# A hybrid attention layer on one core: two gate sums, the latents' last steps and the fetches of o's blocks at other places

## The chip, the cores and the metric

The kernel runs on one core of a Trainium2 chip. The metric is the device time of one execution in microseconds (us). A core has a matrix engine (TensorE, PE, with its weight loads as PEld), three engines for elementwise work (VectorE or DVE, ScalarE or ACT, GpSimd or POOL) and SyncE (SP), which here issues most of the DMA transfers. Each engine works through its own list of instructions in order; semaphores make one wait for another. PE adds its products up in banks of PSUM, and a bank can be written anew only when its last reader is done.

## The reference

The layer has 512 tokens of width 2048, in float32: RMSNorm, one wide input projection, two groups of eight attention heads side by side (MLA with latents of width 768 and 512 and a shared rotary key of 64; FoX with a forget gate), a SiLU gate on each group, one output projection, RMSNorm and the residual.

```python
h = _rms_norm(x, g_pre)
proj = h @ w_in
(q_lat, kv_lat, k_rope_raw, gate_mla,
 fq, fk, fv, f_logit, gate_fox) = jnp.split(proj, split_points, axis=-1)
o_mla = _mla_branch(q_lat, kv_lat, k_rope_raw, g_q, w_uq, g_kv, w_ukv, cos, sin) * jax.nn.silu(gate_mla)
o_fox = _fox_branch(fq, fk, fv, f_logit, b_forget) * jax.nn.silu(gate_fox)
o = jnp.concatenate([o_mla, o_fox], axis=-1) @ w_out
return x + _rms_norm(o, g_post)
```

In the MLA branch the latents are normalised (`_rms_norm(q_lat, g_q)`, `_rms_norm(kv_lat, g_kv)`) and projected to queries of 8 x 192 and to keys and values of 8 x 256; causal softmax attention follows in blocks of 128 queries.

## The kernel before

**Arithmetic.** Every float32 operand is split into a high and a low part that PE takes (`split`, `divide`: a cast on ACT, L129 or L249, then a subtraction on DVE, L130 or L250), and a product is three matmuls, high by high, high by low and low by high (`mm3`, L138 to L140). Weights come in chunks of 128 x 1024. `chunk(i)` hands out chunk i, has chunk i+4 loaded and chunk i+2 divided. There are three buffers each for raw chunks, high parts (`whi`) and low parts (`wlo`). Some chunks come in two parts, `raw` and `second`, which DVE adds ahead of the division (L246).

**Block products.** The columns of the input projection that make the latents ("l", 512 wide) and the MLA gate ("m") are computed by a scheme in the manner of Strassen and Winograd: seven products of half blocks (p1, p2, p4, q6, g5, g7, g3) whose operands are blocks of x (after RMSNorm) and of the weights, or sums of them. The sums of x's blocks were written to memory before. `fetches(n, "m")` issues four loads of 256 KB from there on SP (L908), one per function; the tiles are called `bmg`. `divisions(n, "m")` splits each of them in two. A product is given a list `side`, from which one function is taken every second step of eight; the rest of that list is emptied at the product's end. The output projection is done in the same manner, over the attention's result o; its blocks a11 and a12 come back from memory as `boa`, two loads of 256 KB each, the same L908.

**The order of the stages.** p1, p2 and p4 each for l and m in turn; then q6, g5, g7, g3 for l (504 to 551 us), then the same four for m (551 to 598 us). After that come four pairs of MLA heads, p = 0 to 3. For each pair the queries are projected (`mq`), then keys and values (`mk`, `mv`). The attention of the pair's two heads is put off: its steps (scores of four query blocks, tiles `sm`, exponentials `pm` by L621, transposes `ptm`, values `pvm`) run between the projection steps of the next pair. The output projection follows at about 739 us.

**What sets the order around the change.** Put-off work waits in a queue, `todo`; `pump(n)` takes n functions from it at each step of a product, where n is the product's `rate`. `drain()` runs all that is left. The latents' last steps (scales of their RMSNorm, `latent_part`, L1181) and the gate's parts go through this queue. The gate's sums (`scaled`, L1233, tiles `gc`) combine a product's two banks with an earlier sum, on DVE, and free the banks. `gate(f)` transposes a sum on PE into a bank `gmt` and computes the SiLU. From the program in this order the framework makes each engine's list, and takes an instruction earlier than it is written where it expects it to be ready; so an instruction can stand well ahead of its place in the code. The banks are four for projections (tag pj), three for scores and transposes (at) and one for values (pv).

Of the kernel before, what the change touches and what calls it, by code (L numbers as in the profile page):

```python
# [63 lines left out]
def tile_hybrid_layer(  # L64
# [37 lines left out]
    def proj_bank(name):  # L102
        return bank("pj", name, 4)
# [371 lines left out]
    def drain():  # L475
        while todo:
            todo.popleft()()
# [3 lines left out]
    def set_pace(n):  # L481
        state.update(pace=n, tiles=0)
# [432 lines left out]
    def divisions(n, of):  # L915
        return [lambda j=j: part_fetched(n, of, j) for j in range(2 if of == "o" else 4)]

    def along(a, b):
        return [lambda x=x, y=y: (x(), y()) for x, y in zip(a, b)]

    def fetches(n, of):
        return [lambda j=j: fetch(n, of, j) for j in range(2 if of == "o" else 4)]

    def operand(n, of):
        def parts(kk, t):
            return [oper[n, of][kk // 2][:, x, kk % 2, t * P : (t + 1) * P] for x in range(2)]

        return parts
# [269 lines left out]
    def x_block(half, tokens):  # L1198
        def parts(kk, t):
            ts = slice((tokens + t) * P, (tokens + t + 1) * P)  # L1200
            return hh[8 * half + kk][:, ts], hl[8 * half + kk][:, ts]

        return parts
# [5 lines left out]
    def sums_wide(n):  # L1209
        return lambda kk: [oper[n, "m"][kk // 2][:, x, kk % 2, :] for x in range(2)]  # L1210
# [19 lines left out]
    def scaled(to, o, t0, add, op=ALU.add, col=hcol):  # L1230

        for t in range(2):
            dve.scalar_tensor_tensor(  # L1233
                out=to[:, t, :], in0=o[t], scalar=col[:, t0 + t : t0 + t + 1], in1=add[:, t, :], op0=ALU.mult, op1=op
            )
# [30 lines left out]
    raws_of += [slot(f"lat{i}") for i in range(2)]  # L1266
    for t, to in enumerate(lat_block(0, 0)):
        act.copy(to, fold(A[t]))
    product("p2", "m", x_block(1, 0), A2, False, True)
    c11 = slot("gc11")  # L1270
    scaled_copy(c11, A2, 0)
    B, B2 = ([proj_bank(f"gb{n}{t}") for t in range(2)] for n in "lm")
    product("p4", "l", x_wide(1, 2), B, True, True, side=divisions("q6", "m"), turned=True)
    lat_sum(lat_block(0, 1), B, pl)
    product("p4", "m", x_block(1, 2), B2, True, True, side=fetches("g5", "m"))
    c21 = slot("gc21")
    scaled(c21, B2, 2, pb)
    drain()
    C, G = ([proj_bank(f"g{n}l{t}") for t in range(2)] for n in "cd")
    product("q6", "l", sums_wide("q6"), C, True, True, side=along(divisions("g5", "m"), fetches("g7", "m")), turned=True)  # L1280
    raws_of += [slot(f"lat{i}") for i in (2, 3)]
    lat_sum(lat_block(1, 0), C, pl, ALU.subtract)
    product("g5", "l", sums_wide("g5"), G, True, True, side=along(divisions("g7", "m"), fetches("g3", "m")), turned=True)
    lat_sum(lat_block(1, 1), G, pl, ALU.subtract)
    product("g7", "l", sums_wide("g7"), C, False, True, side=divisions("g3", "m"), turned=True)
    lat_sum(lat_block(1, 1), C, lat_block(1, 1))
    lat_less(lat_block(0, 1), C)
    for i in range(4):
        todo.append(lambda i=i: latent(i, raw(i)))
    product("g3", "l", sums_wide("g3"), G, False, True, turned=True)  # L1290
    lat_sum(lat_block(1, 0), G, lat_block(1, 0))
    for i in range(4, 8):
        todo.append(lambda i=i: latent(i, raw(i)))
# [7 lines left out]
    for i in range(10):  # L1301
        todo.append(lambda i=i: latent_part(i))
    C, G = ([proj_bank(f"g{n}m{t}") for t in range(2)] for n in "cd")
    product("q6", "m", operand("q6", "m"), C, True, True)
    c12 = slot("gc12")
    scaled(c12, C, 0, pa, ALU.subtract)
    product("g5", "m", operand("g5", "m"), G, True, True)
    c22 = slot("gc22")
    scaled(c22, G, 2, pb, ALU.subtract)
    product("g7", "m", operand("g7", "m"), C, False, True)  # L1310
    todo.append(lambda: scaled(c21, C, 2, c21, col=ncol))
    todo.append(lambda: scaled(c22, C, 2, c22))
    for f in range(4):
        todo.append(lambda f=f: gate(f, c11, c21))
    product("g3", "m", operand("g3", "m"), G, False, True)
    drain()
    todo.append(lambda: scaled(c12, G, 0, c12))
    for f in range(4, 8):
        todo.append(lambda f=f: gate(f, c12, c22))
    qnh, qnl = zip(*(latents[i] for i in range(6)))  # L1320
# [2 lines left out]

    for p in range(4):
        c = mla[p]
        if p == 1:
            for f in (*fetches("a11", "o"), *fetches("a12", "o")):
                f()
        if p == 2:
            todo.extendleft([*divisions("a11", "o"), *divisions("a12", "o")])  # L1330
        qb = [proj_bank(f"mq{p}{i}") for i in range(3)]

        proj_T(c["q"], [(qb[i], P, cols(i * P)) for i in range(3)], qnh, qnl, rate=2)
        q = [[split(qb[i], f"mq{p}{i}", SC_M, first=P)] for i in range(2)]
        wholes = slot(f"mw{p}")
        qw = [[whole_block(wholes, i, qb[i], SC_M)] for i in range(2)]
        a, b = rotate(qb[2], P, SC_M, f"q{p}")
        for i in range(2):
            r = tmp(f"rq{p}{i}")
            src = slice(ROPE * i, ROPE * (i + 1))  # L1340
            for half in range(2):
                dve.tensor_tensor(
                    out=r[ROPE * half : ROPE * (half + 1), :], in0=a[src, :], in1=b[src, :], op=ALU.add
                )
            q[i].append(split(r, f"rq{p}{i}", first=P))
            qw[i].append(whole_block(wholes, 4 + i, r))
        if p == 0:
            set_pace(2)
        kb = [proj_bank(f"mk{p}{i}") for i in range(2)]
        vb = [proj_bank(f"mv{p}{i}") for i in range(2)]  # L1350

        def v_cols(w, j):
            return w[:, j, :].rearrange("p (h c) -> p h c", h=2)[:, :, NOPE:]

        kk = 0
        for i in c["kv"]:
            hi, lo = chunk(i)
            for j in range(chunks[i][3]):
                fst, lst = kk == 0, kk == KVR // P - 1
                for n in range(2):  # L1360
                    w = cols(256 * n)
                    mm3(kb[n], w(hi, j), w(lo, j), knh[kk], knl[kk], fst, lst)
                for t in range(NT):
                    o = vb[t // 2][:, (t % 2) * 256 : (t % 2) * 256 + 256]
                    ts = slice(t * P, (t + 1) * P)
                    mm3(
                        o, knh[kk][:, ts], knl[kk][:, ts], v_cols(hi, j), v_cols(lo, j),
                        fst and t % 2 == 0, lst, skip_group_check=True,
                    )
                kk += 1  # L1370
# [16 lines left out]
        enqueue_scores(heads)  # L1387
        enqueue_values(heads)
        done += heads
# [218 lines left out]
```

## Time and profile before

| | us |
|---|---|
| median of 3 runs (914.35 to 918.75) | 918.18 |
| the profiled execution | 916.44 |
| its span, from the first to the last instruction | 914.5 |
| PE busy | 898.6 |
| DVE busy | 626.4 |
| ACT busy | 423.6 |
| POOL busy | 80.5 |
| mean granted clock of PE (1 is full) | 0.996 |

The rows that follow come from the profile of one execution. Times are us from the start of the span unless they are marked ns. A group row names the line, the engine, the operation, the tiles out and in (without numbers), the shapes and the count; then the busy time, the mean ns of one, and the time that the engine was idle just before, with what ended it. A row of the list of waits names the waiting engine and line, the instruction that ended the wait, and the total, the number and the longest. The chain of waits follows the program back from a moment: each row is a start, a duration and what took it. "x8" is a count; SPq is SP's queue of issues. Durations of matmuls overlap, so that PE's pace is read from start to start.

### The profile page before, as it was taken

The numbers are of one execution on the slowest core, as the hardware profiler recorded it, in microseconds if no ns is written. First come the engines' busy times: TensorE is split into PE (matmuls) and PEld (weight loads), VectorE is DVE, ScalarE is ACT, GpSimd is POOL, SyncE is SP. The second block draws the span as 40 slices with busy tenths as digits, with TensorE's granted clock in tenths as the row PEclk, the third lists the DMA queues.
The fourth block names the chain that finished last, engine by engine and source line by source line (L and its number), as shares of the span: only waits on it lengthen the run. The fifth ranks groups of instructions, "written<-read, shape, count | busy, mean of one in ns | idle before, by whom it ended". The sixth has DMA issues, their size and how long they took to land.

```text
span 914.5 us, 12937 instructions
## 1 busy us (share of the span) xinstructions
PE 898.6 (98%) x4732; PEld 774.3 (85%) x4732; DVE 626.4 (69%) x1074; ACT 423.6 (46%) x779; POOL 80.5 (9%) x97
## 2 busy tenths in 40 slices
PE   9999999999999999999999999998999999999997
PEld 8988888898889887888998998877888888888885
DVE  3476878447472764573767777987968896886585
ACT  5772434243221432242554546554554566654473
POOL 1010111111121011011100000001111000000021
PEclk9999999999999999999999999999999999999999
DMA  9378888997997898989789965549999436787878
GB/s 302 93 201 214 232 215 193 239 228 193 225 273 183 199 253 208 235 209 223 249 303 302 305 195 171 163 125 260 206 231 223 119 118 199 239 257 221 271 193 251
DMA packets 121364, 199.40 MB, mean 218 GB/s; under 512 B 16050, under 2 KB 59596, under 8 KB 121300
## 3 DMA queue, kind: packets, MB, share of 16 engines
q1 hardware_dynamic: 105044, 158.84, 55.4%
q0 software_dynamic: 15520, 39.33, 23.4%
q8 instruction: 37, 0.61, 0.3%
q10 hardware_dynamic: 736, 0.40, 0.1%
q14 instruction: 27, 0.22, 0.1%
HBM read 186.46 MB, written 70.80 MB: 281 GB/s over the span
## 4 chain that ended last, share of the span: by engine, by line
PE 55%; DVE 4%; DMA 2%; ACT 1%; issue 0%; SPq 0%; DVEq 0%; ACTq 0%
PE sm L604 2%; PE mq L138 2%; PE mq L140 2%; PE mq L139 2%; PE oa L140 2%; PE oa L138 2%; PE oa L139 2%; PE od L139 2%; PE oc L139 2%; PE od L138 2%; PE oc L140 2%; PE oc L138 2%; PE od L140 2%; DVE wlo L250 1%; DMA boa<-awayoa 1%; PE ptm L630 1%
## 5 line engine op out<-in xcount | busy, mean ns | idle before, releaser
L250 DVE TENSOR_TENSOR wlo<-raw,whi 128x1024 fp32r<-128x1024 f32 (+3 forms) x205 | 242.8, 1186 | 172.8 <-ACT whi L249 163.5
L249 ACT CAST whi<-raw 128x1024 fp32r<-128x1024 f32 (+3 forms) x205 | 209.2, 1022 | 299.7 <-PE fk L139 52.9
L138 PE MATMUL fq<-h,whi 128*128 128x512 f32 x128 | 52.6, 411 | 0.0
L138 PE MATMUL fg<-h,whi 128*128 128x512 f32 x128 | 50.9, 398 | 0.0
L140 PE MATMUL fq<-h,wlo 128*128 128x512 f32 x128 | 50.3, 393 | 0.0
L140 PE MATMUL fg<-h,wlo 128*128 128x512 f32 x128 | 50.1, 392 | 0.0
L139 PE MATMUL fq<-h,whi 128*128 128x512 f32 x128 | 50.1, 391 | 0.0
L138 PE MATMUL fk<-h,whi 128*128 128x512 f32 x128 | 50.0, 391 | 0.0
L139 PE MATMUL fg<-h,whi 128*128 128x512 f32 x128 | 49.9, 390 | 0.0
L139 PE MATMUL fk<-h,whi 128*128 128x512 f32 x128 | 49.8, 389 | 0.0
L140 PE MATMUL fk<-h,wlo 128*128 128x512 f32 x128 | 49.8, 389 | 0.0
L294 POOL DMA_DIRECT2D t<-in_w_out_dram x16 | 18.5, 1159 | 265.0 <-DMA raw<-in_w_uq_dram 177.0
L140 PE MATMUL fv<-whi,h 128*128 128x256 f32 (+1 forms) x128 | 39.5, 309 | 0.0
L138 PE MATMUL fv<-whi,h 128*128 128x256 f32 (+1 forms) x128 | 39.5, 309 | 0.0
L139 PE MATMUL fv<-wlo,h 128*128 128x256 f32 (+1 forms) x128 | 39.5, 309 | 0.0
L561 PE MATMUL fv<-whi,h 128*128 128x456 f32 x128 | 37.6, 378 | 0.0
L138 PE MATMUL mq<-ln,whi 128*128 128x512 f32 x72 | 29.3, 410 | 1.6 <-DVE gc L1233 1.6
L621 ACT ACTIVATE pf<-sf,stf 128x128 f32<-128x128 f32 (+3 forms) x32 | 16.9, 529 | 27.0 <-DVE stf L619 27.0
L139 PE MATMUL mq<-ln,whi 128*128 128x512 f32 x72 | 28.8, 400 | 0.0
L140 PE MATMUL mq<-ln,wlo 128*128 128x512 f32 x72 | 28.8, 400 | 0.0
L140 PEld LDWEIGHTS fq<-h,wlo 128*128 128x128 f32 x128 | 24.0, 188 | 5.4
L140 PEld LDWEIGHTS fg<-h,wlo 128*128 128x128 f32 x128 | 24.0, 188 | 5.3
(525 smaller groups left out, 2452.9 us busy)
## 6 DMA issues: line engine op xcount, KB each, us to landing
raw<-in_w_in_dram SPq DMA_DIRECT2D x80, 512.0 KB
t<-in_w_out_dram SPq DMA_DIRECT2D x32, 512.0 KB
raw<-t SPq DMA_DIRECT2D x32, 512.0 KB
raw<-in_w_out_dram SPq DMA_DIRECT2D x24, 512.0 KB
t<-in_w_out_dram POOLq DMA_DIRECT2D x16, 512.0 KB, 8.7
t<-t POOLq DMA_DIRECT2D x16, 512.0 KB, 8.0
awaymg<-rmg POOLq DMA_DIRECT2D x8, 512.0 KB, 9.1
raw<-t6l SPq DMA_DIRECT2D x8, 512.0 KB
```

The costliest lines, as they stand in the source:

```text
L138: pe.matmul(o, ah, bh, start=first, stop=False, **kw)
L139: pe.matmul(o, ah, bl, start=False, stop=False, **kw)
L140: pe.matmul(o, al, bh, start=False, stop=last, **kw)
L249: act.copy(hi[:, :m], raw[:, :m])
L250: dve.tensor_tensor(out=lo[:, :m], in0=raw[:, :m], in1=hi[:, :m].bitcast(F32), op=ALU.subtract)
L294: pool.dma_start(to.rearrange("p (k c) -> p k c", k=2), second, accum_op=ALU.add)
L561: pe.matmul(banks[t][:, :n], a[k][:, tss[t]], b[:, j, :], start=k == 0 and m == 0, stop=k == NK - 1 and m == 2,)
L604: pe.matmul(s[:, :nn], a[:, qs], c[:, :nn], start=(i == 0), stop=(i == len(pairs) - 1))
L621: act.activation(p, s[:, :n], AF.Exp, bias=st[:, 0:1], accum_out=st[:, 1:2])
L630: pe.transpose(pt[:, b * P : (b + 1) * P], self.p[b][:, n0 : n0 + P], ident)
```

## The change

Four things move; no arithmetic is added or taken away.

1. The fetches and divisions of x's sums are shifted by two: the first two fetches of g5 stand in p2's gate half (`f5[:2]`), the other two and the first two divisions with the first two fetches of g7 in q6 l, and so on, until the last two divisions of g3 stand in g3 l. Before, all four of g5 stood in p4's gate half.
2. The product q6 m takes two functions from `todo` at a step, where it took one.
3. The gate's sums with g7 m and g3 m are computed directly behind their products, where they went through `todo`.
4. The fetches of o's blocks a11 and a12 are issued at the start of pair 3, before at the start of pair 1; their divisions enter `todo` behind pair 3's query projection, before at the start of pair 2.

```diff
-    product("p2", "m", x_block(1, 0), A2, False, True)
+    d5, d7, d3 = (divisions(n, "m") for n in ("g5", "g7", "g3"))
+    f5, f7, f3 = (fetches(n, "m") for n in ("g5", "g7", "g3"))
+    product("p2", "m", x_block(1, 0), A2, False, True, side=f5[:2])
...
-    product("p4", "m", x_block(1, 2), B2, True, True, side=fetches("g5", "m"))
+    product("p4", "m", x_block(1, 2), B2, True, True)
...
-    product("q6", "l", sums_wide("q6"), C, True, True, side=along(divisions("g5", "m"), fetches("g7", "m")), turned=True)
+    product("q6", "l", sums_wide("q6"), C, True, True, side=[*f5[2:], *along(d5[:2], f7[:2])], turned=True)
...
-    product("g3", "l", sums_wide("g3"), G, False, True, turned=True)
+    product("g3", "l", sums_wide("g3"), G, False, True, side=d3[2:], turned=True)
...
-    product("q6", "m", operand("q6", "m"), C, True, True)
+    product("q6", "m", operand("q6", "m"), C, True, True, 2)
...
     product("g7", "m", operand("g7", "m"), C, False, True)
-    todo.append(lambda: scaled(c21, C, 2, c21, col=ncol))
-    todo.append(lambda: scaled(c22, C, 2, c22))
+    scaled(c21, C, 2, c21, col=ncol)
+    scaled(c22, C, 2, c22)
     for f in range(4):
         todo.append(lambda f=f: gate(f, c11, c21))
     product("g3", "m", operand("g3", "m"), G, False, True)
+    scaled(c12, G, 0, c12)
     drain()
-    todo.append(lambda: scaled(c12, G, 0, c12))
...
-        if p == 1:
+        if p == 3:
             for f in (*fetches("a11", "o"), *fetches("a12", "o")):
                 f()
-        if p == 2:
-            todo.extendleft([*divisions("a11", "o"), *divisions("a12", "o")])
...
+        if p == 3:
+            todo.extendleft([*divisions("a11", "o"), *divisions("a12", "o")])
```

(g5 l and g7 l change in the same way as q6 l.)

**Blocks of o, on ACT.** This is ACT's list before, where pair 1's query projection begins; `pm` is the exponential of a score block of pair 0, `mv0h` and `mv` are pair 0's values.

```order
L129 CAST mv0h_5923<-mv_5818 128x256
L129 CAST mv0h_5925<-mv_5819 128x256
L129 CAST boa_5935<-boa_5935 128x512
L1031 COPY mv_5927<-mv_5819 128x256
L129 CAST boa_5937<-boa_5937 128x512
L621 ACTIVATE pm_5967,stm_5965<-sm_5961,stm_5965 128x128
L129 CAST boa_5939<-boa_5939 128x512
L621 ACTIVATE pm_5980,stm_5978<-sm_5971,stm_5978 128x256
L129 CAST boa_5941<-boa_5941 128x512
L249 CAST whi_6027<-raw_5868 128x1024
L621 ACTIVATE pm_6002,stm_6000<-sm_5993,stm_6000 128x384
```

In the list after, this is ACT where pair 3's query projection begins; `pm` and `mv` are pair 2's.

```order
L129 CAST mv2h_6759<-mv_6601 128x256
L633 COPY pdm_6748<-ptm_6746 128x128
L129 CAST boa_6769<-boa_6769 128x512
L129 CAST boa_6771<-boa_6771 128x512
L129 CAST boa_6773<-boa_6773 128x512
L1031 COPY mv_6761<-mv_6601 128x256
L129 CAST boa_6775<-boa_6775 128x512
L621 ACTIVATE pm_6801,stm_6799<-sm_6795,stm_6799 128x128
L249 CAST whi_6858<-raw_6669 128x1024
L621 ACTIVATE pm_6814,stm_6812<-sm_6805,stm_6812 128x256
```

The casts of boa have left the exponentials of pair 0, and all four now stand ahead of the first exponential of pair 2, where two stood ahead of the first of pair 0.

**Blocks of o, on SP.** Before, at the end of pair 2 (`t` is work for the output projection's weights, raw from in_w_ukv pair 3's key and value weights):

```order
L297 DMA t_168<-in_w_out_dram 128x2x512
L299 DMA t_160<-whi_6668 1x16
L234 DMA raw_6666<-in_w_ukv_dram 128x2x512
L297 DMA t_160<-in_w_out_dram 128x2x512
L234 DMA raw_6788<-in_w_ukv_dram 128x2x512
L299 DMA t_164<-whi_6790 1x16
L234 DMA raw_6864<-in_w_out_dram 128x2x512
L297 DMA t_164<-in_w_out_dram 128x2x512
```

After, at the same place:

```order
L297 DMA t_168<-in_w_out_dram 128x2x512
L234 DMA raw_6669<-in_w_ukv_dram 128x2x512
L234 DMA raw_6780<-in_w_ukv_dram 128x2x512
L299 DMA t_160<-whi_6671 1x16
L908 DMA boa_6769<-awayoa_4132 128x512
L908 DMA boa_6771<-awayoa_4005 128x512
L908 DMA boa_6773<-awayoa_4146 128x512
L908 DMA boa_6775<-awayoa_4025 128x512
L297 DMA t_160<-in_w_out_dram 128x2x512
L234 DMA raw_6856<-in_w_out_dram 128x2x512
```

The four fetches stand behind both loads of in_w_ukv, and one 512 KB load of `t` that stood between these two now stands behind the fetches.

**Fetches of x's sums, on DVE.** Before, in p2's gate half and p4's first half (`wlo` with `whi` are the low parts of weight chunks, raw with second the sums of chunks in two parts, `bmg` the blocks of x's sums):

```order
L250 TENSOR_TENSOR wlo_4373<-raw_4312,whi_4372 128x1024
L246 TENSOR_TENSOR raw_4348<-raw_4348,second_4350 128x1024
L250 TENSOR_TENSOR wlo_4394<-raw_4348,whi_4393 128x1024
L246 TENSOR_TENSOR raw_4368<-raw_4368,second_4370 128x1024
L246 TENSOR_TENSOR raw_4388<-raw_4388,second_4390 128x1024
L250 TENSOR_TENSOR wlo_4415<-raw_4368,whi_4414 128x1024
L250 TENSOR_TENSOR wlo_4443<-raw_4388,whi_4442 128x1024
L246 TENSOR_TENSOR raw_4409<-raw_4409,second_4411 128x1024
L250 TENSOR_TENSOR wlo_4478<-raw_4409,whi_4477 128x1024
```

After, at the same place:

```order
L250 TENSOR_TENSOR wlo_4375<-raw_4312,whi_4374 128x1024
L246 TENSOR_TENSOR raw_4348<-raw_4348,second_4350 128x1024
L130 TENSOR_TENSOR bmg_4368<-bmg_4368 128x512
L250 TENSOR_TENSOR wlo_4398<-raw_4348,whi_4397 128x1024
L246 TENSOR_TENSOR raw_4370<-raw_4370,second_4372 128x1024
L130 TENSOR_TENSOR bmg_4390<-bmg_4390 128x512
L250 TENSOR_TENSOR wlo_4419<-raw_4370,whi_4418 128x1024
L246 TENSOR_TENSOR raw_4392<-raw_4392,second_4394 128x1024
L250 TENSOR_TENSOR wlo_4447<-raw_4392,whi_4446 128x1024
L246 TENSOR_TENSOR raw_4413<-raw_4413,second_4415 128x1024
L250 TENSOR_TENSOR wlo_4482<-raw_4413,whi_4481 128x1024
```

Two low parts of bmg stand between the additions and low parts of the chunks that p4 uses.

**Gate sums, on DVE.** Before, at the end of g3 m (`lat` and `ln` are the latents and their parts, `gc` the gate's sums, `gm` the gate):

```order
L130 TENSOR_TENSOR ln_5583<-lat_4805,ln_5583 128x512
L1181 SCALAR_TENSOR_TENSOR lat_3743<-lat_3743,gcol,ls 128x512
L250 TENSOR_TENSOR wlo_5602<-raw_5538,whi_5601 128x768
L130 TENSOR_TENSOR ln_5593<-lat_3743,ln_5593 128x512
L1181 SCALAR_TENSOR_TENSOR lat_3743<-lat_3743,gcol,ls 128x512
L1233 SCALAR_TENSOR_TENSOR gc_4661<-gcm_5210,ncol,gc_4661 128x512
L1233 SCALAR_TENSOR_TENSOR gc_4661<-gcm_5211,ncol,gc_4661 128x512
L130 TENSOR_TENSOR ln_5612<-lat_3743,ln_5612 128x512
L250 TENSOR_TENSOR wlo_5626<-raw_5567,whi_5625 128x768
L1233 SCALAR_TENSOR_TENSOR gc_5443<-gcm_5210,hcol,gc_5443 128x512
L1233 SCALAR_TENSOR_TENSOR gc_5443<-gcm_5211,hcol,gc_5443 128x512
L1251 SCALAR_TENSOR_TENSOR gm_5643<-gm_5643,gmt_5644 128x512
```

After, in g3 m:

```order
L130 TENSOR_TENSOR ln_5515<-lat_3743,ln_5515 128x512
L1181 SCALAR_TENSOR_TENSOR lat_3743<-lat_3743,gcol,ls 128x512
L250 TENSOR_TENSOR wlo_5543<-raw_5492,whi_5542 128x1024
L130 TENSOR_TENSOR ln_5531<-lat_3743,ln_5531 128x512
L1233 SCALAR_TENSOR_TENSOR gc_4657<-gcm_5210,ncol,gc_4657 128x512
L1233 SCALAR_TENSOR_TENSOR gc_4657<-gcm_5211,ncol,gc_4657 128x512
L1233 SCALAR_TENSOR_TENSOR gc_5463<-gcm_5210,hcol,gc_5463 128x512
L1233 SCALAR_TENSOR_TENSOR gc_5463<-gcm_5211,hcol,gc_5463 128x512
L250 TENSOR_TENSOR wlo_5568<-raw_5518,whi_5567 128x1024
L1251 SCALAR_TENSOR_TENSOR gm_5577<-gm_5577,gmt_5578 128x512
L1251 SCALAR_TENSOR_TENSOR gm_5577<-gm_5577,gmt_5591 128x512
L250 TENSOR_TENSOR wlo_5604<-raw_5540,whi_5603 128x1024
```

The four gc that read g7's banks stood among the low parts of pair 0's query weights (768 columns). Now they stand ahead of all of these, and ahead of the last two low parts of 1024 columns.

More of the change, by code (lines that the diff above doesn't have):

```diff
@@ L1279, in tile_hybrid_layer @@
     C, G = ([proj_bank(f"g{n}l{t}") for t in range(2)] for n in "cd")
-    product("q6", "l", sums_wide("q6"), C, True, True, side=along(divisions("g5", "m"), fetches("g7", "m")), turned=True)
+    product("q6", "l", sums_wide("q6"), C, True, True, side=[*f5[2:], *along(d5[:2], f7[:2])], turned=True)
     raws_of += [slot(f"lat{i}") for i in (2, 3)]
     lat_sum(lat_block(1, 0), C, pl, ALU.subtract)
-    product("g5", "l", sums_wide("g5"), G, True, True, side=along(divisions("g7", "m"), fetches("g3", "m")), turned=True)
+    product("g5", "l", sums_wide("g5"), G, True, True, side=[*along(d5[2:], f7[2:]), *along(d7[:2], f3[:2])], turned=True)
     lat_sum(lat_block(1, 1), G, pl, ALU.subtract)
-    product("g7", "l", sums_wide("g7"), C, False, True, side=divisions("g3", "m"), turned=True)
+    product("g7", "l", sums_wide("g7"), C, False, True, side=[*along(d7[2:], f3[2:]), *d3[:2]], turned=True)
     lat_sum(lat_block(1, 1), C, lat_block(1, 1))
```

## The prediction

> **What bounds the kernel now.** I read the page first, then the list of waits of TensorE, then the chain of waits around each entry of that list, and last the table of stretches with their clock. The page says that TensorE is the bound:
>
> ```profile
> span 914.5 us, 12937 instructions
> PE 898.6 (98%) x4732; PEld 774.3 (85%) x4732; DVE 626.4 (69%) x1074; ACT 423.6 (46%) x779; POOL 80.5 (9%) x97
> ```
>
> The program's matrix work does not change, so all that an edit of this kind can win is the time in which PE waits or runs at a lower clock. The list of waits (who waited for what, us in total, times, longest) is short:
>
> ```profile
> PE sm L604 <- ACT pm L621: 2.6, 1, 2.6
> PE mix L1450 <- ACT scaler L1449: 1.9, 1, 1.9
> PE mq L138 <- DVE gc L1233: 1.6, 1, 1.6
> PE gbm L139 <- DVE wlo L250: 1.3, 2, 0.8
> PE xt L423 <- DMA xa<-in_x_dram: 1.1, 1, 1.1
> PE pvf L139 <- DVE plf L130: 0.9, 1, 0.9
> ```
>
> The waits on xt and mix are the program's start and end, which the change does not touch. Three lie in its reach: sm (scores of latent pair 0, run in pair 1's q projection), mq (start of pair 0) and gbm (product p4's gate half). The first is the dearest. The chain of waits there (start, us, what) is:
>
> ```profile
> 625.71 8.54 DMA boa<-awayoa
> ...
> 634.28 0.62 ACT boa L129
> ...
> 635.68 0.37 ACT pm L621 x2
> 636.10 1.77 PE sm L604 x5
> 637.86 0.43 PE mq L138
> ...
> 640.93 0.23 PE mq L140
> ```
>
> A block of o (boa) takes 8.54 us to land. Its cast stands on ACT ahead of the first exponential (pm), ACT works in order, and PE waits for the bank that this exponential frees. A matmul of mq, 0.23 us at the full clock (the last row), takes 0.43 right after the wait. The table of stretches (start:end, length, busy us and count of PE, PEld, DVE, ACT and POOL, granted clock, DMA share, GB/s) says why:
>
> ```profile
> 597.00:600.50 3.50, 2.34 (x16) 1.71 (x14) 3.50 (x6) 3.13 (x4) 0.00 (x0) 1.00 0.44 152
> 600.50:604.00 3.50, 3.10 (x16) 2.59 (x17) 3.50 (x6) 1.79 (x4) 0.00 (x0) 1.00 0.55 152
> ...
> 633.44:636.85 3.41, 0.82 (x4) 0.67 (x4) 1.13 (x3) 2.57 (x8) 0.00 (x0) 1.00 1.11 313
> 636.85:640.27 3.42, 3.42 (x10) 2.60 (x10) 3.32 (x9) 1.66 (x5) 0.00 (x0) 0.52 0.91 250
> ```
>
> PE was busy for 0.82 of 3.41 us, and in the next 3.42 us the clock was 0.52, which costs 3.42 x 0.48 = 1.64 us. After the wait at mq (1.16 us idle of 3.50) the clock stayed at 1.00. So a gap of 2.6 us in one stretch of 3.4 cost a half clock, and one of 1.2 did not.
>
> **The change, part by part.** The sum is made against the profiled execution: 916.44 us, of which 914.5 are the span. The median of the runs shown is 918.18, 1.74 above it.
>
> *Blocks of o leave pair 1.* The four fetches, casts and low parts go, and with them both costs: 2.6 + 1.64 = **-4.2 us**. What is late next there is the exponential itself. Pair 2, which has no such fetch in its q projection, shows how little that is:
>
> ```profile
> 667.00:702.00 35.00, 34.62 (x197) 30.25 (x198) 26.94 (x61) 16.24 (x42) 5.07 (x5) 1.00 0.96 226
> 702.00:739.00 37.00, 37.00 (x215) 32.12 (x213) 32.03 (x67) 19.14 (x49) 1.66 (x2) 1.00 0.59 138
> ```
>
> It idles 0.38 us in 35. If pair 1 idled as much, 0.2 to 0.4 of the 4.2 would come back; pair 2 gets as much since its queue loses the four divisions that stood at its head, so I take **-0.2** for the two together, within -0.4 and +0.4.
>
> *Blocks of o arrive in pair 3.* By the order shown above, the same thing is rebuilt there: SP issues the four fetches behind a kv weight load, and ACT has all four casts ahead of the first exponential of pair 2's scores, where before only two stood ahead of it. Three of the low parts stand ahead of its maximum on VectorE. Rows for the timing:
>
> ```profile
> L234 SPq DMA_DIRECT2D raw<-in_w_ukv_dram x2: 395/395/395, 695.7 to 698.6; - x2
> L908 SPq DMA_DIRECT2D boa<-awayoa x4: 558/634/901, 625.7 to 628.1; - x4
> L129 ACT CAST boa<-boa x6: 606/618/622, 634.3 to 747.5; 128x512 fp32r<-128x512 f32 x6
> L130 DVE TENSOR_TENSOR boa<-boa x6: 673/680/693, 635.7 to 750.6; 128x512 fp32r<-128x512 f32 x6
> L619 DVE TENSOR_REDUCE stm<-sm x24: 279/484/680, 630.2 to 719.9; 128x1 f32<-128x128 f32 x6, 128x1 f32<-128x256 f32 x6, 128x1 f32<-128x384 f32 x6, 128x1 f32<-128x512 f32 x6
> ...
> 710.54 0.87 PE L604 MATMUL sm<-mk,mq 128*128 128x512 f32 x3
> t<-in_w_out_dram POOLq DMA_DIRECT2D x2, 512.0 KB, 9.4
> 699.00:709.00 10.00, 10.00 (x65) 8.66 (x65) 7.45 (x17) 5.53 (x16) 1.98 (x2) 1.00 0.97 224
> ```
>
> The second kv load is issued at 698.6 for 0.4 us. Four fetches at 0.634 each follow, so the fourth is issued at about 700.9. With the 8.54 us of pair 1 it lands at 709.4. Then come its cast 0.62, its low part 0.68, the maximum 0.28, the exponential 0.37 and an estimated 0.25 for handing over between engines five times (0.03 between the first two rows of the chain above), 2.2 together: the bank is free at 711.6. PE wants it at 710.54, the fourth score block, and the work of PE ahead of that block is the same in both orders. That is a wait of **+1.1 us**. The ends: the fourth lands 1.1 us earlier or better, and the wait is 0; or it takes the 9.4 us that the 512 KB transfers take there, and the wait is 1.9. I stay with the middle, since the DMA engines are as full there (share 0.97) as they were in pair 1. Below zero it cannot go, as pair 3 had no idle time (37.00 of 37.00). VectorE gets 4 x 0.68 = 2.7 us more on 32.03 of 37 us, and ACT 2.5 us on 19.14: both fit.
>
> *Fetches and divisions of x's sums two earlier.* Two fetches of 256 KB now lie in p2's gate half, between the two-part weight loads (raw and second) that product p4 needs, and their splits lie among p4's. Rows of p4, its two halves, VectorE's and ACT's groups in them, and the chain that ended the later wait:
>
> ```profile
> 480.00:492.00 12.00, 12.00 (x99) 11.88 (x99) 8.31 (x7) 4.89 (x6) 0.00 (x0) 1.00 0.93 321
> 492.00:505.00 13.00, 11.53 (x49) 8.68 (x48) 12.00 (x14) 6.46 (x9) 0.00 (x0) 1.00 0.89 294
> ...
> L250 DVE TENSOR_TENSOR wlo<-raw,whi 128x1024 fp32r<-128x1024 f32 x8 | 9.7, 1223 | 2.5 <-ACT whi L249 2.4
> L246 DVE TENSOR_TENSOR raw<-raw,second 128x1024 f32<-128x1024 f32 x6 | 7.3, 1223 | 2.7 <-DMA second<-in_w_in_dram 2.7
> L130 DVE TENSOR_TENSOR bmg<-bmg 128x512 fp32r<-128x512 f32 x4 | 2.5, 686 | 0.0
> L249 ACT CAST whi<-raw 128x1024 fp32r<-128x1024 f32 x9 | 9.3, 1048 | 15.3 <-DVE raw L246 14.6 <-DMA raw<-t6l 0.7
> ...
> 491.60 6.04 DMA second<-in_w_in_dram
> ...
> 497.73 1.23 DVE raw L246
> 498.96 1.15 DVE wlo L250
> ```
>
> A chunk of p4 goes through add 1.22, cast 1.05 and low part 1.22 in series, 3.5 us, and PE idles 1.47 us in the second half. Two more low parts on VectorE are 1.4 us, and two fetches are 0.52 MB at 321 GB/s, 1.6 us of full DMA engines. Hidden, they cost 0, since the first half has 3.7 us of VectorE free; in series they cost 3.0. The four fetches that leave p4's gate half cannot pay for it, as they were issued behind the last second load there. The rows are nearer to the hidden end (in the first half PE never waited), so I take **+1.0**.
>
> *Gate sums directly behind their products, and the latents' steps two a tile.* The rows of the wait at mq:
>
> ```profile
> 576.00:600.00 24.00, 23.34 (x109) 19.11 (x107) 23.77 (x33) 15.29 (x20) 0.00 (x0) 1.00 0.56 159
> ...
> 599.23 0.87 DVE wlo L250
> 600.10 0.67 DVE gc L1233
> ```
>
> PE waited 1.6 us for a bank that VectorE's last gc freed. In the new order all four gc of g7 stand in g3's time, so that wait goes. But VectorE is full there (23.77 of 24.00), and the four gc now stand ahead of weight low parts that PE needs, so these become late next. The latents' products by their scales move into q6's time, where the list has no wait of PE; PE's own products cover them, and they cost nothing unless the scales are late, which falls under the upper end below. Ends: -1.6 when no low part is late, +0.8 when one of 0.87 us is late by its whole length beyond today's wait. I take **-0.7**, nearer to the relief, because both moves take work out of the full stretch.
>
> Sum: -4.2 - 0.2 + 1.1 + 1.0 - 0.7 = **-3.0 us**. That is 913.4 for the profiled execution, and 918.18 - 3.0 = 915.2 for the median; I say 915.
>
> A rule of the Trainium skill bears on the clock term. The page "TensorE: Matmul & The Clock Gate", section "HAM oscillation — how this bites in real kernels", asks for no idle gap of PE above about 3.4 us, a whole window; by that, pair 3 could wait up to 3.4 us without a lower clock, and pair 1's wait of 2.6 should not have lowered it. The trace disagrees: its window had 0.82 us of work in it, and the next ran at 0.52. By the page the sum would be -1.4 in place of -3.0.
>
> **Rivals.** *All is won* (0.25): the blocks of o land in time in pair 3, p4 hides the fetches, the wait at mq goes: -4.2 - 0.2 - 1.6 = -6.0, 912.2. For it speaks that a 512 KB transfer of SP that stood ahead of the second kv load in pair 3 now stands behind the fetches. *The wait only moves* (0.15): the fourth block takes 10.1 us or more, the wait reaches 2.6 in one window, and the half clock follows: 2.6 + 1.64 = 4.2 in place of 1.1, sum +0.1, 918.3. For it speaks the 224 GB/s of that stretch. *p4 becomes the slow place* (0.12), which makes the kernel slower: second loads issued one chunk later meet the full DMA engines. It costs the whole 3.0, the excess of the serial 3.5 us over PE's 3.0 for a chunk (12.00 us for the four of the first half) four times over, 2.0, and a half clock of 1.64 once the gap passes 2.6 us: 6.6 in place of 1.0, sum +2.6, 920.8. It decides from 4.0 us lost in p4 on, where the sum is zero. Against it speaks that the first half never waited. *The half clock of pair 1 has another cause and stays* (0.05): 1.64 of the gain is lost, sum -1.4, 916.8. Against it speaks the stretch with 0.82 us of work right ahead of it. This is what the page named above would make of that stretch.
>
> **How the numbers follow.** The forecast holds 0.40, with its own range 912.5 to 917.5; 0.03 is for what I have not seen. About 0.5% (4.6 us) is what a measurement of this kernel can tell from no change. Below 913.6 lie 0.22 of "all is won" and 0.08 of the forecast: faster 0.30. Above 922.8 lies the upper part of "p4 becomes the slow place", of a wait in pair 3 beyond 2.6 beside it, and the unseen: slower 0.13. The rest, 0.57, is within. The range reaches from 910.5, 1.7 below "all is won", to 921, the price of the slow p4.
>
> **What would show it.** In the list of waits sm <- pm should be gone from 633 and a shorter one should stand near 710, with boa in its chain; the stretch after it should show a clock of 1.00. mq <- gc should be gone, with wlo or nothing in its place; gbm <- wlo should be between 1.3 and 3. I am wrong if pair 3 shows a clock near 0.5, if p4 idles over 4 us, or if pair 1 still waits.

## The result and the profile after

The changed kernel takes 912.14 us (median of 11 runs, 910.95 to 915.41) against 917.92 us for the kernel before (11 runs, 914.07 to 921.71). The ratio, which is estimated from all these runs and is not the quotient of the two medians (they lie 5.8 us apart), is 0.995, with a 95% interval of 0.9929 to 0.9971: about 4.6 us, or 0.5%, faster, and between 2.7 and 6.5 us by the interval. In the experiments further below, two executions of 3819 and 2310 us were far slower than all others and are left out of the ratios. The forecast was 915 us within 910.5 to 921, and 3.0 us of gain.

The page of the changed kernel, and its list of waits of TensorE (who waited for what, us in total, times, longest):

```profile
span 910.4 us, 12934 instructions
PE 898.7 (99%) x4732; PEld 774.3 (85%) x4732; DVE 625.2 (69%) x1074; ACT 424.6 (47%) x779; POOL 80.9 (9%) x97
```

```profile
PE mix L1452 <- ACT scaler L1451: 1.9, 1, 1.9
PE xt L423 <- DVE wlo L250: 1.3, 1, 1.3
PE gbm L139 <- DVE wlo L250: 1.1, 2, 0.6
PE warm L157 <- DVE warm L152: 1.1, 1, 1.1
PE sm L604 <- ACT pm L621: 1.0, 1, 1.0
PE gdm L139 <- DVE wlo L250: 0.7, 1, 0.7
```

PE's busy time is the same (898.6 and 898.7 us), and the span is 4.1 us shorter. The wait of mq for gc is gone and one of gdm for a low part has come; the wait of sm for pm has gone from 2.6 to 1.0 us. Where it lies now shows in the table of stretches (start:end, length, busy us and count of PE, PEld, DVE, ACT and POOL, granted clock, DMA share, GB/s), first the changed kernel's and then two rows of the kernel before that the prediction did not need:

```profile
492.00:505.00 13.00, 11.88 (x53) 8.80 (x53) 10.63 (x10) 5.03 (x5) 0.00 (x0) 1.00 0.76 260
576.00:600.00 24.00, 23.34 (x111) 18.81 (x110) 24.00 (x33) 15.30 (x21) 0.00 (x0) 1.00 0.49 142
600.00:627.00 27.00, 27.00 (x150) 23.27 (x149) 19.67 (x29) 11.28 (x23) 2.08 (x2) 1.00 0.76 182
627.00:651.00 24.00, 24.00 (x125) 20.28 (x124) 19.36 (x49) 12.45 (x32) 3.95 (x4) 1.00 1.04 263
667.00:702.00 35.00, 34.97 (x203) 30.53 (x202) 27.78 (x59) 17.66 (x43) 5.24 (x5) 1.00 0.95 226
702.00:739.00 37.00, 35.91 (x203) 30.87 (x201) 32.74 (x69) 20.95 (x51) 1.65 (x2) 1.00 0.54 143
```

```profile
600.00:627.00 27.00, 26.09 (x146) 22.46 (x147) 22.18 (x33) 12.47 (x25) 2.08 (x2) 1.00 0.61 147
627.00:651.00 24.00, 21.41 (x101) 17.72 (x100) 17.20 (x46) 12.55 (x31) 3.10 (x3) 0.93 0.90 237
```

Length less PE's busy time is PE's idle time of a stretch. The two profiled executions compare like this:

| stretch | idle before | idle after | difference | forecast |
|---|---|---|---|---|
| p4, gate half (492 to 505) | 1.47 | 1.12 | -0.35 | +1.0 |
| g7, g3 and pair 0 (576 to 627) | 0.66 + 0.91 | 0.66 + 0.00 | -0.91 | -0.7 |
| pair 1 (627 to 651), wait | 2.59 | 0.00 | -2.59 | -2.6 |
| pair 1, lower clock | 1.64 | 0.00 | -1.64 | -1.64 |
| pair 2 (667 to 702) | 0.38 | 0.03 | -0.35 | -0.2 |
| pair 3 (702 to 739) | 0.00 | 1.09 | +1.09 | +1.1 |

The sum is -4.75 us. The span shows -4.1, since the changed kernel's execution was 0.6 us late before it came to any changed place, which the first starts of gate products show (before, then after; the last two times are the first and last start):

```profile
L138 PE MATMUL gm<-whi,h x32: 389/389/396, 447.2 to 479.8; 128*128 128x512 f32 x32
```

```profile
L138 PE MATMUL gm<-whi,h x32: 389/389/396, 447.8 to 480.5; 128*128 128x512 f32 x32
```

In pair 3 the wait is the one forecast, by place and size, but its chain is not quite. From the timelines of SP, ACT, DVE and PE after (start, us, instruction, idle time before it in brackets):

```profile
L908 SPq DMA_DIRECT2D boa<-awayoa x4: 344/493/702, 693.4 to 695.0; - x4
...
702.20 0.62 ACT L129 CAST boa<-boa 128x512 fp32r<-128x512 f32 x1 [1.55 <-DMA boa<-awayoa]
...
703.79 0.63 ACT L129 CAST boa<-boa 128x512 fp32r<-128x512 f32 x1
...
702.85 0.69 DVE L130 TENSOR_TENSOR boa<-boa 128x512 fp32r<-128x512 f32 x1 [3.11 <-ACT boa L129]
703.46 0.68 DVE L652 TENSOR_TENSOR gm<-pvm,gm 128x512 f32<-128x512 f32 x1
704.06 0.68 DVE L130 TENSOR_TENSOR boa<-boa 128x512 fp32r<-128x512 f32 x1
704.66 0.29 DVE L606 TENSOR_TENSOR sm<-sm,mask 128x128 f32<-128x128 f32 x1
704.86 0.68 DVE L130 TENSOR_TENSOR boa<-boa 128x512 fp32r<-128x512 f32 x1
705.46 0.28 DVE L619 TENSOR_REDUCE stm<-sm 128x1 f32<-128x128 f32 x1
...
705.77 0.37 ACT L621 ACTIVATE pm<-sm,stm 128x128 f32<-128x128 f32 x1 [1.35 <-DVE stm L619]
...
706.28 0.96 PE L604 MATMUL sm<-mk,mq 128*128 128x512 f32 x3 [1.02 <-ACT pm L621]
```

The fourth fetch is issued at 695.0 and its cast begins at 703.79, 8.8 us later. Its low part, the maximum and the exponential follow, and PE has waited 1.02 us for the bank. But the fourth block is not what came last. Its cast ends at 704.42, and then ACT idles 1.35 us until VectorE has the maximum. VectorE starts at 702.85, when the second block's cast has ended, and works without a gap until the maximum at 705.46: a low part, the product of an earlier head's result with its gate (gm), a low part, the mask of a score block (sm) and a low part. By the semaphores that they wait for, the three low parts are those of the second, third and fourth block, and the fourth block's starts 0.44 us after its cast has ended. So the last step of this wait is the order on VectorE, with three low parts ahead of the maximum. The four other profiles with o's blocks fetched at the start of pair 2 or 3 look the same: ACT idles 1.0 to 1.5 us for the maximum there. In pair 1 it was otherwise: the exponential followed directly behind ACT's second cast.

### The profile page after: what moved, and what is told of

It is laid out like the page before. It is cut to its first block, busy times and chain, and to the rows that moved or that the text cites. A ratio compares the mean times of both kernels' runs of the same rounds, so it can differ in the third digit from the quotient of the medians.

```text
span 910.4 us, 12934 instructions
## 1 busy us (share of the span) xinstructions
PE 898.7 (99%) x4732; PEld 774.3 (85%) x4732; DVE 625.2 (69%) x1074; ACT 424.6 (47%) x779; POOL 80.9 (9%) x97
## 4 chain that ended last, share of the span: by engine, by line
PE 92%; DVE 4%; DMA 2%; ACT 1%; issue 1%; SPq 0%; ACTq 0%; DVEq 0%
PE fv L561 4%; PE fg L138 3%; PE fq L140 3%; PE fq L138 3%; PE fq L139 3%; PE fg L140 3%; PE fg L139 3%; PE fk L139 3%; PE fk L140 3%; PE fk L138 3%; PE sm L604 3%; PE fv L140 2%; PE fv L138 2%; PE fv L139 2%; PE mq L138 2%; PE mq L140 2%
## 5 line engine op out<-in xcount | busy, mean ns | idle before, releaser
L140 PEld LDWEIGHTS fk<-h,wlo 128*128 128x128 f32 x128 | 24.0, 188 | 5.0
```

What stands on the lines that cost most here:

```text
L140: pe.matmul(o, al, bh, start=False, stop=last, **kw)
```

## The experiments

All times of an experiment are ratios to runs of the kernel before on the same chip, with a 95% interval. One per mille is 0.9 us.

**The four parts apart.** Four kernels split the change. The first undoes the fourth part:

```diff
-        if p == 3:
+        if p == 1:
             for f in (*fetches("a11", "o"), *fetches("a12", "o")):
                 f()
+        if p == 2:
+            todo.extendleft([*divisions("a11", "o"), *divisions("a12", "o")])
...
-        if p == 3:
-            todo.extendleft([*divisions("a11", "o"), *divisions("a12", "o")])
```

> The changed kernel with its fourth part undone: the blocks of o are fetched at the start of pair 1 and their divisions enter at pair 2, as before; the other three parts stay. Theory (the gain lies in the wait for o's blocks): the wait of sm for pm comes back near 633 us with 2.4 to 2.8 us, the stretch of 3.4 us behind it runs at a clock near 0.5, pair 3 has no wait, and the whole is about 3.5 us longer than the changed kernel, 1.2 us shorter than the kernel before (ratio 0.9987). Rival (the gain lies in the gate's sums and the earlier fetches): it keeps the changed kernel's time, ratio 0.995. Second rival (the half clock has another cause than the wait): the wait comes back and the clock stays at 1.0, ratio 0.997.

Measured: 0.9982 (0.9966 to 0.9998). The wait in pair 1 came back, in two pieces, and the clock stayed at 1.00:

```profile
PE sm L604 <- ACT pm L621: 2.4, 2, 1.2
...
627.00:651.00 24.00, 21.64 (x111) 18.01 (x110) 19.15 (x50) 12.63 (x31) 3.95 (x4) 1.00 0.91 245
```

The gain of the whole change does not stay without the fourth part. The missing half clock is taken up below.

The second is the kernel before with the fourth part alone (the same edit the other way round).

> The kernel before with the fourth part alone: o's blocks fetched at the start of pair 3, divided behind its query projection. Theory: pair 1 has neither wait nor lower clock, pair 3 has a wait of sm for pm of about 1.0 us behind boa, mq still waits 1.6 us for gc and gbm 1.3 us for wlo; 3.5 us shorter than the kernel before, ratio 0.9962. Rival (the gain lies in the other parts): ratio 0.999 to 1.000.

Measured: 0.9970 (0.9956 to 0.9984), 2.75 us. Pair 1 has no wait and pair 3 one of 1.8 us. In this profile p4's gate half waited 2.9 us in one piece, and there the next stretch ran at half clock:

```profile
PE gbm L139 <- DVE wlo L250: 2.9, 1, 2.9
...
PE sm L604 <- ACT pm L621: 1.8, 1, 1.8
PE mq L138 <- DVE gc L1233: 1.6, 1, 1.6
...
496.08:499.49 3.41, 1.02 (x5) 0.52 (x3) 1.93 (x2) 0.71 (x2) 0.00 (x0) 1.00 1.01 369
499.49:502.90 3.41, 2.93 (x7) 2.35 (x8) 3.17 (x4) 3.04 (x6) 0.00 (x0) 0.52 0.64 204
```

By this estimate the fourth part is the largest of the four, hardly ahead of the gate parts (2.6 us, below). The 3.5 us expected lie inside its interval of 1.5 to 4.0 us.

The third is the kernel before with the first part alone (the `side` lists of the diff).

> The kernel before with the first part alone: fetches and divisions of x's sums two earlier. Theory, from the trace after: the four fetches that leave p4's gate half make room there, PE's idle time in 492 to 505 us falls from 1.5 to 1.1 us, and the time is within 1 us of the kernel before, ratio 0.9995. Rival (the prediction's term): the splits and fetches lengthen p4's chain by 1.0 us, ratio 1.001. The rest as in the kernel before: sm waits 2.6 us at 633 with a half clock behind it, mq 1.6 us.

Measured: 0.9992 (0.9978 to 1.0006). No gain or loss can be told from it, and p4's gate half idled 1.57 us in this profile. The prediction's +1.0 us (1.0011) lies outside the interval. The wait in pair 1 was 3.0 us here, the longest of all, and still no half clock followed:

```profile
637.22 0.97 PE L604 MATMUL sm<-mk,mq 128*128 128x512 f32 x3 [2.98 <-ACT pm L621]
...
632.00:635.41 3.41, 2.24 (x11) 1.67 (x10) 0.00 (x0) 0.01 (x1) 0.81 (x1) 1.00 1.05 399
635.41:638.82 3.41, 1.60 (x7) 1.33 (x8) 1.98 (x6) 3.41 (x10) 0.00 (x0) 1.00 1.12 266
638.82:642.23 3.41, 2.46 (x14) 1.96 (x13) 3.30 (x9) 1.45 (x3) 0.00 (x0) 1.00 0.63 201
```

The fourth is the kernel before with the second and third part alone (q6 m at rate 2, `scaled` directly behind g7 m and g3 m).

> The kernel before with the second and third part alone: q6 m takes two steps from the queue, the gate's sums stand directly behind g7 m and g3 m. Theory: mq no longer waits for gc (1.6 us), gdm waits for a weight's low part instead (0.7 us), 0.9 us shorter, ratio 0.999. Rival: low parts late by more than the relief, ratio 1.000 to 1.001. In both the wait of sm for pm at 633 stays with its half clock.

Measured: 0.9972 (0.9956 to 0.9989), 2.6 us, more than expected. mq no longer waits and gdm waits 0.7 us, as in the theory. But pair 1 also changed: its wait fell to two pieces of 1.07 and 0.95 us. The chain there, of this kernel and of the one with the first part alone (whose gate sums stand as before), suggests why:

```profile
624.39 7.00 DMA boa<-awayoa
...
600.00:627.00 27.00, 27.00 (x150) 23.24 (x149) 18.96 (x28) 12.21 (x24) 2.08 (x2) 1.00 0.76 186
```

```profile
626.46 8.92 DMA boa<-awayoa
...
600.00:627.00 27.00, 25.43 (x141) 21.72 (x141) 22.20 (x32) 12.59 (x23) 2.08 (x2) 1.00 0.57 142
```

With the gate's sums early, 186 GB/s of loads pass in pair 0 in place of 142, and o's first block then takes 7.00 us in place of 8.92. The two other profiles with o's blocks in pair 1 agree: 147 GB/s and 8.54 us in the kernel before, 185 GB/s and 7.1 us in the one with the fourth part undone. So a stage's relief went together with a shorter wait in the next stage. That the loads are the link between the two is read from these four profiles; no run changed them alone.

**The wait and the place of o's blocks.** The next kernels ran beside the changed kernel itself, on one chip.

> The changed kernel once more, on the chip and beside the runs of the kernel before that the next three share: ratio 0.995, a wait of sm for pm of about 1.0 us near 705, no half clock.

Measured: 0.9954 (0.9936 to 0.9972); sm waits 0.5 us in this profile, and no half clock follows.

In the next, o's blocks are fetched behind pair 3's query projection and divided behind its key and value products, so that their casts leave the place ahead of the exponentials:

```diff
-        if p == 3:
-            for f in (*fetches("a11", "o"), *fetches("a12", "o")):
-                f()
...
         if p == 3:
-            todo.extendleft([*divisions("a11", "o"), *divisions("a12", "o")])
+            for f in (*fetches("a11", "o"), *fetches("a12", "o")):
+                f()
...
+        if p == 3:
+            todo.extend([*divisions("a11", "o"), *divisions("a12", "o")])
         drain()
         values_into(v_pair(f"mv{p}"), slice(0, 256), [piece_of(vb, t, 256)[0] for t in range(NT)])
```

> The changed kernel with the blocks of o fetched behind pair 3's query projection and divided behind its key and value products, so that their casts stand behind the last exponential of pair 2's scores. Theory (the wait in pair 3 is the casts standing ahead of the first exponential): sm no longer waits for pm, pair 3 idles under 0.2 us, and the output projection, which needs the blocks at about 734, does not wait; 1.0 us shorter than the changed kernel, ratio 0.994. Rival (the exponentials are late there for another reason, as VectorE is fuller in pair 3): a wait of about 1 us stays. Second rival: the blocks come late for the output projection, and oa waits.

Measured: 0.9940 (0.9920 to 0.9961). The wait is gone (the stretch of pair 3 and the whole list of waits), and oa does not wait:

```profile
702.00:739.00 37.00, 37.00 (x212) 32.10 (x212) 33.81 (x69) 23.35 (x55) 1.65 (x2) 1.00 0.53 149
```

```profile
PE mix L1452 <- ACT scaler L1451: 1.9, 1, 1.9
PE gbm L139 <- DVE wlo L250: 1.2, 3, 0.5
PE warm L157 <- DVE warm L152: 1.1, 1, 1.1
PE gdm L139 <- DVE wlo L250: 0.7, 1, 0.7
```

VectorE is fuller here (33.81 of 37 us) than in the changed kernel (32.74), so how full it is was not the cause. The casts on ACT and the low parts on VectorE moved together in this kernel, so that it cannot tell which of them held the exponential; the trace of pair 3 further above puts the last step on the low parts. The time is 1.3 us below that of the changed kernel beside it, which the intervals do not separate; the wait itself is gone in the profile.

The other direction is one pair earlier (`if p == 2` ahead of the fetches, divisions as changed).

> The changed kernel with the fetches of o's blocks at the start of pair 2, their divisions as in the changed kernel. Theory (the wait goes where the fetches go): sm waits 1 to 3 us for pm near 667, behind boa, pair 3 has no wait, and the time is that of the changed kernel within 2 us, ratio 0.994 to 0.998; where the idle time of one 3.41 us stretch reaches 2 us, the next runs at half clock. Rival (pair 2 hides the fetches, as its loads come earlier): no wait in pair 2 or 3, ratio 0.994.

Measured: 0.9996 (0.9980 to 1.0011): no gain is left, which is outside the 0.994 to 0.998 expected. The wait is 2.0 us long, now in pair 2, and the half clock follows it:

```profile
667.00:702.00 35.00, 32.97 (x180) 28.21 (x180) 30.40 (x67) 18.27 (x47) 5.07 (x5) 0.95 0.84 190
...
666.87:670.28 3.41, 1.40 (x8) 1.03 (x7) 3.41 (x10) 1.93 (x6) 1.13 (x1) 1.00 0.62 168
670.28:673.70 3.42, 3.42 (x10) 2.69 (x9) 3.31 (x9) 1.61 (x5) 0.85 (x1) 0.52 0.97 161
```

The lower clock is not that of the profiled execution alone: the mean granted clock over this kernel's twelve runs is 0.9951, near the 0.9953 of the kernel before and below the 0.9973 of the changed kernel on this chip. So the wait goes where the fetches go, in pairs 1, 2 and 3, and it vanishes when the casts and low parts stand behind the exponentials.

**What the gate parts are worth by themselves.** This is the kernel with o's blocks late, but with the gate's sums and q6 m's rate as in the kernel before.

> O's blocks late (fetched behind pair 3's query projection, divided behind its key and value products), x's sums two earlier as changed, but the gate's sums and the latents' steps as in the kernel before. It asks why the gate parts alone gained 2.2 us where their own stage shows 0.9. Theory (they also shortened pair 1's wait for o's blocks, from a latency of 8.5 us to 7.0, and with it the half clock): with no such blocks in pair 1 they are worth 0.9 us, so this is 0.9 us longer than the same kernel with them, ratio 0.995; mq waits 1.6 us for gc, gdm does not wait. Rival (they are worth the whole 2.2 us by themselves): ratio 0.9965.

Measured: 0.9932 (0.9917 to 0.9946), faster than either expectation, beside 0.9940 with the gate parts, which was measured on another chip. mq waits its 1.6 us and gdm does not wait, so 0.9 us more of waiting is in the profile (the spans are 907.8 and 906.5), but not in the times. Without o's blocks in pair 1 the gate parts gain nothing that these runs can show, though the intervals leave room for 0.9 us. Of their 2.6 us in the kernel before, the profiles put 0.9 into their own stage and more into pair 1, which idled 0.6 us less and lost the 1.64 us of lower clock.

**p4 and the fetches of x's sums.** The first two fetches of g5 stand in p4's gate half in place of p2's:

```diff
-    product("p2", "m", x_block(1, 0), A2, False, True, side=f5[:2])
+    product("p2", "m", x_block(1, 0), A2, False, True)
...
-    product("p4", "m", x_block(1, 2), B2, True, True)
+    product("p4", "m", x_block(1, 2), B2, True, True, side=f5[:2])
```

> The changed kernel with the first two fetches of g5 in p4's gate half in place of p2's gate half; the rest as changed. By the prediction's term (two fetches and splits in p2 and p4 lengthen p4's chain by 1.0 us) p4 idles 0.1 to 0.5 us in place of 1.1, and it is 0.7 us shorter than the changed kernel. Rival, from the trace after (p4's loads gain by what leaves p4's gate half): p4 idles about as much as in the changed kernel or more, 1.1 to 1.5 us.

Measured: 0.9939 (0.9917 to 0.9961), p4's gate half idling 1.07 us where the changed kernel beside it idles 1.15. The same edit on top of the late o blocks:

> Both single edits that came out fastest at once: o's blocks fetched behind pair 3's query projection and divided behind its key and value products, and the first two fetches of g5 in p4's gate half. Theory: no wait of sm, p4 idles about 1.1 us, gdm waits 0.7; ratio 0.993 to 0.994. Rival (the two fetches in p4's gate half cost something that the earlier run hid in its spread): ratio 0.995.

Measured: 0.9934 (0.9918 to 0.9951). Here p4's gate half idled 2.0 us in one piece, and a half clock followed in the profile. The first part undone, on top of the late o blocks:

> O's blocks late and the gate parts as changed, but the fetches and divisions of x's sums as in the kernel before. Theory, from the traces (p4 idles 1.5 to 2.9 us with four fetches in p4's gate half, 1.0 to 1.6 us with the change): 0.7 us longer than the same kernel with the shifted fetches, ratio 0.995, p4 idling 1.3 to 1.9 us. Rival, the prediction's term: 1.0 us shorter, ratio 0.993.

Measured: 0.9940 (0.9921 to 0.9960), p4's gate half idling 1.98 us. The times of these kernels cannot be told apart. In the profiles there is a pattern on VectorE, in the group of the additions of two-part chunks in p4 (idle time before them last). First the changed kernel's, then that of the kernel before with the fourth part alone:

```profile
L246 DVE TENSOR_TENSOR raw<-raw,second 128x1024 f32<-128x1024 f32 x7 | 8.5, 1218 | 0.1
```

```profile
L246 DVE TENSOR_TENSOR raw<-raw,second 128x1024 f32<-128x1024 f32 x6 | 7.3, 1225 | 3.5 <-DMA second<-in_w_in_dram 3.4
```

In the seven profiles with the two fetches spread over p2's gate half, VectorE waited 0.0 to 0.4 us for second loads; in the six others 0.9 to 3.5 us. The last kernel (o's blocks late) issues both fetches ahead of p2's gate half, to part the traffic from the order that it brings about:

```diff
-    product("p2", "m", x_block(1, 0), A2, False, True, side=f5[:2])
+    for f in f5[:2]:
+        f()
+    product("p2", "m", x_block(1, 0), A2, False, True)
```

> O's blocks late, the gate parts as changed, and the first two fetches of g5 both ahead of p2's gate half, where the change spreads them over it. In the seven kernels that spread them, VectorE waits 0.0 to 0.4 us for second loads in p4; in the six others it waits 0.9 to 3.5 us. Here the traffic has left p4's gate half as in the seven, but VectorE's list again has two additions of two-part chunks in a row with a low part behind them, as the six have (their first pair one chunk earlier). If the traffic decides, VectorE waits under 0.5 us for second loads and p4 idles 1.0 to 1.2 us; if VectorE's order decides, it waits 0.9 us or more. The time in either case: ratio 0.993 to 0.995.

Measured: 0.9937 (0.9916 to 0.9959). VectorE waited 0.8 us, and p4 idled 1.09 us in its first half and 0.50 in its second. That lies between the two expectations. There is a third candidate. On SP's list of this kernel one second load stands ahead of its raw load, once. This is also so in all six kernels whose VectorE waited 0.9 us or more, and in none of the seven where it waited 0.4 us or less. The traffic is the weakest of the three: in all six, SP issued the fetches of p4's gate half behind p4's last second load (496.65 behind 491.60 in the kernel before). No run changed SP's order alone, so which one decides stays open; nothing of it shows in the time.

## Why the prediction was right

The time, the sign and the largest terms came out. Point by point:

- *Blocks of o leave pair 1* (-4.2 us): the wait and the lower clock are both gone in the profile after. That the wait belongs to o's blocks is shown: it followed the fetches to pair 2 and pair 3. But the lower clock is not a fixed part of it. Two later kernels had waits of 2.4 us (in two pieces) and 3.0 us in pair 1 at full clock. So the step that took the 1.64 us of one profiled execution as a property of the kernel was too sure for a single execution. In the mean it holds. Every run has its mean granted clock on record: on one chip 0.9953 for the kernel before (19 runs, 0.992 to 0.999) and 0.9973 for the changed kernel (6 runs, 0.996 to 0.998). The difference, 0.0020 of 914 us, makes an estimated 1.8 us.
- *Blocks of o arrive in pair 3* (+1.1): measured 1.02 us in the first profile, 0.5 in the second, 1.8 with the fourth part alone. Issue times and the place came out earlier than worked out (695.0 for the fourth issue), as most is earlier by then. That 1.02 came so near to 1.1 is in part luck. The fourth issue stood 10.3 us ahead of PE's need, where the step had 9.6; the time from issue to cast was 8.8 us, where it had 8.54; and from the cast to the free bank went 2.5 us, where it had 2.2. The step's chain of one block's cast and low part left out the work that stands between the low parts on VectorE. The range of 0 to 1.9 was right.
- *p4* (+1.0): this term failed. The step took two splits and two fetches as work that is partly in series with p4's chunks. In the profile after, the stretch idles 0.35 us less, and VectorE hardly waits for second loads (0.1 us, before 2.7). The times of the kernels with and without the shift do not differ. The reason for the sign is not settled, as told above.
- *Gate sums* (-0.7): the profile shows -0.91, and gdm's wait of 0.7 us for a low part is what the step named as late next. What the step left out is pair 1: alone, the parts gained 2.6 us (1.0 to 4.0) in the kernel before, and nothing measurable where pair 1 has no blocks of o; the profiles put the difference into pair 1's wait and clock. In the whole change the fourth part removes that wait anyway, so the two gains should not add. The times agree (2.75, 0.7 and 2.6 us alone, 4.6 together), but their intervals are too wide to show it.
- *Pair 2* (-0.2): -0.35.

Of the rivals, "all is won" failed by pair 3's wait, though its time, 912.2, came nearest to the median: p4 took 1.35 us less than forecast. By the ratio the gain of 4.6 us lies between its 6.0 and the 3.0 forecast. "The wait only moves" is what happens with the fetches in pair 2. The rival that the half clock has another cause than the wait is out: the idle time within a stretch tells, in every profile, whether the next stretch is slowed (last section), and in the kernels that waited in pair 1 at full clock the idle time came in two pieces, or was cut in two by the stretch's border.

The kernels with o's blocks late came out a little faster than the change itself: 0.9940, and 0.9934 (on another chip) with two fetches in p4's gate half, against 0.9954. The intervals overlap, so the times do not show this; the profiles show the wait gone.

## What to carry to other kernels

A load that nobody needs for 100 us can still stop the critical engine, if the in-order list of a helper engine has its consumer ahead of urgent work: look at the order on every engine that takes part (here ACT in pair 1 and VectorE in pair 3), and put the consumers behind the urgent work, rather than the load elsewhere. A wait found in one profile should be split into its idle time, which came back in every profile here, and a lower clock behind it, which depends on where the idle time falls. Gains of parts need not add when one part shortens the wait that another removes.

## What the runs showed of the hardware

The clock was lowered by idle time in a fixed stretch of 3.41 us, and the whole of a stretch need not be idle. Three more rows, the first from the kernel with o's blocks late and two fetches in p4's gate half, the others from the start and the end of the one with the first part undone; each is followed by the row of the next stretch:

```profile
497.90:501.31 3.41, 1.41 (x6) 1.05 (x6) 3.36 (x4) 2.32 (x3) 0.00 (x0) 1.00 0.40 131
501.31:504.73 3.42, 3.42 (x10) 2.60 (x9) 2.33 (x4) 1.76 (x3) 0.00 (x0) 0.52 0.89 283
```

```profile
4.16:7.57 3.41, 1.58 (x14) 1.42 (x13) 1.47 (x3) 1.59 (x5) 0.00 (x0) 1.00 0.94 290
7.57:10.98 3.41, 3.41 (x21) 3.08 (x20) 1.29 (x2) 1.41 (x3) 0.00 (x0) 1.00 1.06 375
...
898.45:901.86 3.41, 1.54 (x5) 0.58 (x4) 2.17 (x8) 1.55 (x5) 2.31 (x2) 1.00 0.55 206
901.86:905.27 3.41, 2.05 (x2) 0.48 (x2) 1.69 (x3) 0.60 (x2) 0.00 (x0) 0.52 0.96 359
```

With 1.87 us or more of the stretch idle (1.87 and 2.00 here, 2.01 in pair 2, 2.39 and 2.59 elsewhere) the next stretch had 0.52; with 1.83 us or less (1.83 here, 1.81 in the kernel with the first part alone, whose wait of 2.98 us was cut by a border) it kept 1.00. All fourteen profiles, cut into such stretches from end to end, have no exception: 16 whole stretches idle 1.87 us or more, and each is followed by one at 0.52; the other 3688 idle 1.83 us or less, and none of them is followed by a lowered clock. The stretches follow each other every 3.41 us, and their borders lie elsewhere in each execution (496.08, 497.90 and 632.00 above are not whole stretches apart), so that the same wait can cost 1.64 us more in one execution than in another. The Trainium skill, page "TensorE: Matmul & The Clock Gate", section "What's actually happening", gives a free-running window of 3413 ns, and the trace agrees with that length; its idle window as the condition for the lower clock is stricter than what these rows show.
